# Two experts of a mixture form their second product in rows, both at the end of the order, and the last normalization's work on the vector engine is put elsewhere

## The chip, the core and the metric

The kernel runs on one core of one Trainium2 chip. The metric is the device time of one execution in microseconds (us); of three runs the median counts. In the trace the engines are PE (matrix products, with PEld for its weight loads), DVE (vector work), ACT (activations and scaled copies), POOL and SP; SP starts most of the transfers (DMA), POOL the gathers, the scatters and a few others.

## What is computed

The reference is a trunk of two layers on 512 tokens of width 1024. Each layer is a mixer (sparse attention beside a short convolution) and a feed-forward part, each followed by a residual and a normalization of the rows. The second layer's feed-forward part is a mixture of eight experts, two for each token, and it is the only part that the change touches:

```python
def swiglu(h, wg, wu, wd):
    return (jax.nn.silu(h @ wg) * (h @ wu)) @ wd

def moe_swiglu(h, w_router, wg, wu, wd):
    logits = (h @ w_router).astype(jnp.float32)
    top_v, top_i = lax.top_k(logits, TOP_K)
    w_top = jax.nn.softmax(top_v, axis=-1)
    gate = jnp.sum(jax.nn.one_hot(top_i, N_EXPERTS, dtype=jnp.float32) * w_top[..., None], axis=-2)
    out = jnp.zeros_like(h)
    for e in range(N_EXPERTS):
        out = out + gate[..., e:e + 1].astype(h.dtype) * swiglu(h, wg[e], wu[e], wd[e])
    return out
...
h = layer_norm(ALPHA * h + f, ln2_g[l], ln2_b[l])
```

`wg` and `wu` are 1024 x 1408 and `wd` is 1408 x 1024 for each expert, all in float32: 17.3 MB for an expert.

## The kernel before

The experts are sorted by how many tokens chose them. Expert number e of this order has room for `CAPS[e]` tokens (L28: 160, 168, 152, 144, 136, 132, 128, 128), and `TURN` (L29) says in which order they are worked on: 0, 5, 1, 6, 2, 4, 3, 7. An expert of up to 128 tokens is one chunk of rows, a larger one is two (`chunks`, L33).

For each expert the tokens' rows are fetched from memory by POOL (`gather`, L773) and turned on PE so that the features lie on the partitions (`gather_t`, L783). The weights come in blocks of up to 1 MB that SP loads (`eblock`, L799) into a ring of nine buffers, three called `stage` and six called `estage`. Each block is split into two float16 parts (`split16_ops`, L820): ACT writes the high part `whi` (L824), then DVE the low part `wlo` (L825). The split parts have four buffers each. A product is three matrix instructions (`mm3`, L191: high by high, high by low, low by high), so that 792 instructions do one expert.

The hidden width of 1408 is 11 groups of 128, taken as six and five. A turn of the loop in `moe` (L969 to L1009) runs in this order: the gate product of the first six (`expert_up`, "mm"; four blocks), then what is left of the expert before (`end`), the up product of the first six ("tr"; four blocks), the gate product of the last five (three blocks), the second product over the first six groups (`expert_down`, L869, "s"; three blocks), and the up product of the last five (three blocks). `expert_gate` (L854) and `expert_hidden` (L860) form the hidden values `eg`, `ehh`, `ehl` on ACT and DVE.

`expert_down` holds 128 x 128 of the weights as the stationary operand and moves the tokens past it: 264 instructions for an expert, each as wide as the expert has tokens. So its result lies with the features on the partitions and must be turned back: `expert_end` (L883) copies it out of PSUM with a scale into `yt`, and `expert_out` (L895) makes eight (or sixteen) transposes on PE, scales them by the tokens' gates on ACT into `yr`, and POOL adds these rows to `abuf` in memory (L910). The adds to `abuf` follow each other.

The last expert is treated apart. Once the adds of all others have landed, SP loads all 512 rows of `abuf` into `h` (L984), and POOL fetches the last expert's own rows into `xl` (L985). While its products run, DVE computes the statistics of the rows in `h` (L995, L919; the block stands in program order behind the splits of the second product's first half, so ahead of those of the last up group), and scales them (L925, L926), after which SP stores them. The rows of the last expert get its contribution on DVE (L906), statistics, scaling, and POOL scatters them over the output (L1030). A flag for tokens beyond the room that was kept is read just ahead of that.

The program's order on each engine is a list that a scheduler makes ahead of the run, by the order of the source and its own estimate of when each operand is there; `issue_after(x)` adds that nothing of the block under it stands ahead of x on x's engine. The engines then work strictly down their lists.

Of the kernel before, what the change touches and what calls it, by code (L numbers as in the profile page):

```python
# [7 lines left out]
F32 = mybir.dt.float32  # L8
# [4 lines left out]
AF = mybir.ActivationFunctionType  # L13
OP = mybir.AluOpType
# [14 lines left out]
TURN = (0, 5, 1, 6, 2, 4, 3, 7)  # L29
# [3 lines left out]
def chunks(e):  # L33

    c = CAPS[e]
    return [(0, c)] if c <= 128 else [(0, CH), (CH, c - CH)]

# [12 lines left out]
class Trunk:  # L50
# [698 lines left out]
    def slot_data(self, e):  # L749
# [17 lines left out]
        nc.vector.tensor_reduce(self.sgate[0:n, e, 0:nh], x[:, :, 2:5], axis=AX.X, op=OP.add)  # L767

# [113 lines left out]

    def expert_end(self, e, ys):  # L883
# [11 lines left out]
    def expert_out(self, e, yt, last=None):  # L895
        nc, mp = self.nc, self.mp
        for r, (s, n) in enumerate(chunks(e)):
            yr = None if last is not None else mp.tile([128, D], F32, name="yr", bufs=2)[0:n]
            for half in range(2):
# [3 lines left out]
                c = slice(half * 512, half * 512 + 512)  # L903
                g = self.sgate[0:n, e, r:r + 1]
                if last is not None:
                    nc.vector.scalar_tensor_tensor(last[:, r, c], p[0:n], g, last[:, r, c], op0=OP.mult, op1=OP.add)  # L906
                else:
                    nc.scalar.activation(yr[:, c], p[0:n], AF.Copy, scale=g)
            if last is None:
                nc.gpsimd.indirect_dma_start(out=self.abuf[:, :], in_=yr, in_offset=None, compute_op=OP.add,  # L910
                                             out_offset=bass.IndirectOffsetOnAxis(ap=self.dst[0:n, e, r:r + 1], axis=0))
# [16 lines left out]
    def moe(self, l):  # L928
# [30 lines left out]
        nl, nh = chunks(final)[0][1], len(chunks(final))  # L959
        xl = end[0:nl, 2:2 + nh]  # L960
        mv = mp.tile([128, NT, 2], F32, name="mv4")

        def before_last(tts):

            for tt in tts:
                self.rows_scaled(self.h[:, tt], mv[:, tt, 0:1], rs[:, tt], gb)
                self.store(tt)
        end = None
        for turn, e in enumerate(TURN):  # L969
# [6 lines left out]
            if end is not None:  # L976
                end()
            out = (lambda x=TURN[turn - 1]: self.expert_out(x, self.yt)) if turn else None
# [3 lines left out]
            if last:  # L982
                for tt in range(NT):
                    nc.sync.dma_start(self.h[:, tt], self.abuf[tt * 128:(tt + 1) * 128])  # L984
                self.gather_rows(e, xl, self.abuf)  # L985
# [164 lines left out]
```

## Time and profile before

| | us |
|---|---|
| median of three runs | 1389.82 |
| lowest and highest | 1389.7, 1390.5 |
| profiled execution, its own time | 1391.8 |
| profiled execution, span of its instructions | 1389.8 |

| engine | busy in the span |
|---|---|
| PE | 1339.5 us (96%) |
| DVE | 867.3 us (62%) |
| ACT | 670.0 us (48%) |
| POOL | 75.1 us (5%) |

The mixture takes the time from some 910 us to the end. The busy share of PE counts the pipelined ends of its instructions, so that it tells when PE stands still and not how fast it goes. Times in the rows are microseconds from the start of the span; where several instructions are put together, the second number is the time from the first one's start to the last one's end. What stands in brackets behind an instruction is the idle time of its engine just ahead of it, and what ended that.

### The profile page before, as it was taken

The page shows a single profiled execution, that of the slowest core. Times are in us where ns is not written, and L with a number is a line of the kernel's source. Part 1 is how long each engine was busy: PE and PEld are TensorE (multiplying, and loading weights), DVE is VectorE, ACT ScalarE, POOL GpSimd, SP SyncE. Part 2 cuts the span into 40 slices and gives each one's busy share as a digit, 9 for nine tenths or more (in the row PEclk, how much of TensorE's full clock was granted, in tenths as well). Part 3 has the DMA queues.
Part 4 walks back from the last instruction along what each step waited for, and adds up shares of the span by engine and source line. Part 5 has one row for each costly group of instructions (what it writes and reads, how often), then busy time and mean ns, then how long its engine had stood idle before and what let it go on. Part 6 is the DMA issues. An engine that isn't in the chain of part 4 may idle for free.

```text
span 1389.8 us, 27646 instructions
## 1 busy us (share of the span) xinstructions
PE 1339.5 (96%) x11888; PEld 1181.5 (85%) x11888; DVE 867.3 (62%) x1249; ACT 670.0 (48%) x951; POOL 75.1 (5%) x81
## 2 busy tenths in 40 slices
PE   5999999999999999999999999999999999999974
PEld 5887888898888888888888878889999999999974
DVE  7567665843333332228567665769787788778876
ACT  3575544332322322122565444236777677668761
POOL 3000000000000000000000000101101140011010
PEclk9999999999999999999999999999999999999986
DMA  7442021232322322234442021679999999999961
GB/s 249 128 121 62 31 61 61 91 122 72 110 92 90 121 92 91 91 107 110 130 122 62 32 61 61 211 270 321 327 356 334 323 332 389 337 363 353 343 236 75
DMA packets 135810, 241.16 MB, mean 174 GB/s; under 512 B 10810, under 2 KB 80538, under 8 KB 135684
## 3 DMA queue, kind: packets, MB, share of 16 engines
q1 hardware_dynamic: 131444, 225.28, 47.5%
q0 software_dynamic: 4240, 14.07, 3.7%
q8 instruction: 94, 1.54, 0.5%
q14 instruction: 32, 0.26, 0.1%
HBM read 227.74 MB, written 11.68 MB: 172 GB/s over the span
## 4 chain that ended last, share of the span: by engine, by line
PE 91%; DVE 4%; DMA 2%; ACT 1%; issue 1%; SPq 0%; POOL 0%; POOLq 0%; ACTq 0%
PE mm L198 46%; PE s L198 17%; PE tr L198 11%; PE po L481 3%; PE s L499 2%; PE s L465 2%; PE s L373 1%; PE po L198 1%; PE tr L465 1%; PE tr L499 1%; DVE h L925 1%; PE tr L183 1%; DVE h L926 1%; PE mm L677 1%; PE po L475 1%
## 5 line engine op out<-in xcount | busy, mean ns | idle before, releaser
L198 PEld LDWEIGHTS <-whi 128*128 128x128 f16 x4224 | 342.8, 99 | 2.9 <-issue 2.4
L142 ACT ACTIVATE whi<-stage 128x1024 fp32r<-128x1024 f32 x122 | 127.9, 1058 | 304.8 <-PE mm L198 181.7
L143 DVE TENSOR_TENSOR wlo<-stage,whi 128x1024 fp32r<-128x1024 f32 x118 | 143.7, 1223 | 196.6 <-ACT whi L142 194.4
L198 PE MATMUL mm<-xh,whi 128*128 128x512 f32 (+1 forms) x672 | 257.4, 383 | 0.3 <-DVE e L304 0.3
L198 PE MATMUL mm<-xh,wlo 128*128 128x512 f32 (+1 forms) x672 | 253.0, 377 | 0.4 <-DVE wlo L143 0.4
L198 PE MATMUL mm<-xl,whi 128*128 128x512 f32 (+1 forms) x672 | 252.3, 376 | 0.0
L825 DVE SCALAR_TENSOR_TENSOR wlo<-estage,whi 128x1536 f16<-128x1536 f32 (+4 forms) x106 | 201.6, 1919 | 35.2 <-ACT whi L824 34.9
L198 PEld LDWEIGHTS <-wlo 128*128 128x128 f16 x2112 | 208.6, 99 | 13.2 <-DVE wlo L825 13.2
L824 ACT ACTIVATE whi<-estage 128x1536 f16<-128x1536 f32 (+4 forms) x106 | 170.6, 1613 | 68.8 <-PE s L198 28.0
L198 PEld LDWEIGHTS mm<-xh,wlo 128*128 128x128 f32 x672 | 127.1, 189 | 24.0 <-DVE wlo L143 0.6
L198 PEld LDWEIGHTS mm<-xh,whi 128*128 128x128 f32 x672 | 127.6, 190 | 21.6 <-issue 1.3
L198 PEld LDWEIGHTS mm<-xl,whi 128*128 128x128 f32 x672 | 127.3, 189 | 21.1
L198 PE MATMUL tr<-eh,wlo 128*128 128x128 f16 (+6 forms) x704 | 136.2, 228 | 8.3 <-DVE wlo L825 8.3
L198 PE MATMUL s<-ehh,wlo 128*128 128x128 f16 (+6 forms) x704 | 134.7, 228 | 4.5 <-DVE wlo L825 4.5
L198 PE MATMUL tr<-eh,whi 128*128 128x128 f16 (+6 forms) x704 | 136.3, 229 | 0.0
L198 PE MATMUL tr<-el,whi 128*128 128x128 f16 (+6 forms) x704 | 136.2, 228 | 0.0
L198 PE MATMUL s<-ehh,whi 128*128 128x128 f16 (+6 forms) x704 | 134.7, 228 | 1.1 <-ACT ehh L865 1.1
L198 PE MATMUL s<-ehl,whi 128*128 128x128 f16 (+6 forms) x704 | 134.6, 228 | 1.1 <-DVE ehl L866 1.1
L198 PE MATMUL mm<-eh,whi 128*128 128x128 f16 (+6 forms) x704 | 132.7, 226 | 0.0
L198 PE MATMUL mm<-el,whi 128*128 128x128 f16 (+6 forms) x704 | 132.6, 226 | 0.0
L198 PE MATMUL mm<-eh,wlo 128*128 128x128 f16 (+6 forms) x704 | 132.6, 226 | 0.0
L825 DVE SCALAR_TENSOR_TENSOR wlo<-stage,whi 128x1536 f16<-128x1536 f32 (+5 forms) x56 | 103.0, 1842 | 23.2 <-ACT whi L824 22.2
(302 smaller groups left out, 2220.7 us busy)
## 6 DMA issues: line engine op xcount, KB each, us to landing
estage<-in_moe_wd_dram SPq DMA_DIRECT2D x29, 1024.0 KB, 7.7
stage<-in_w_in_dram SPq DMA_DIRECT2D x32, 512.0 KB, 5.1
estage<-in_moe_wu_dram SPq DMA_DIRECT2D x21, 768.0 KB, 10.5
estage<-in_moe_wg_dram SPq DMA_DIRECT2D x18, 768.0 KB, 7.1
stage<-in_ffn_wg_dram SPq DMA_DIRECT2D x11, 1024.0 KB, 5.2
stage<-in_ffn_wu_dram SPq DMA_DIRECT2D x11, 1024.0 KB, 5.2
stage<-in_ffn_wd_dram SPq DMA_DIRECT2D x11, 1024.0 KB, 4.8
stage<-in_moe_wd_dram SPq DMA_DIRECT2D x11, 1024.0 KB, 9.4
```

The costliest lines, as they stand in the source:

```text
L142: nc.scalar.activation(h, st, AF.Copy)
L143: (eng or nc.vector).tensor_tensor(o, st, h.bitcast(F32), op=OP.subtract)
L183: nc.tensor.transpose(p[:, k * 128:(k + 1) * 128], self.h[:, tt, kk * 128:(kk + 1) * 128], self.ident)
L198: self.nc.tensor.matmul(p, a, b, start=first and n == 0, stop=last and n == total - 1, skip_group_check=shared)
L373: nc.tensor.matmul(ph[r:r + 64, 0:256], e2[kv][:, c].rearrange("p g n -> p (g n)"), w1s[c // 8][:, c % 8], start=c < 2, stop=c > 13, skip_ ...
L465: nc.tensor.transpose(q[:, k * 128:k * 128 + 128], flat[:, c:c + 128], self.ident)
L475: nc.tensor.matmul(po, vbd[r], pct[r, la // 2], start=True, stop=False, skip_group_check=True)
L481: nc.tensor.matmul(po[g * 64:g * 64 + 64, i * 128:i * 128 + 128], v[:, j, c:c + 64], flat[:, k:k + 128], start=False, stop=lbr == 1 and j ...
L499: nc.tensor.matmul(sp[:, wide[i]], qs[:, a, g, qi[i]], keys[:, br, g, 0:wide[i].stop - wide[i].start], start=keys is ks and i == blocks[0] ...
L677: self.nc.tensor.matmul(p, self.h[:, tt, k * 128:k * 128 + 128], self.oh32[:, tt], start=tt == 0 and k % 3 == 0, stop=tt == NT - 1 and (k ...
L824: nc.scalar.activation(hi[:, c], st[:, c], AF.Copy, scale=WS)
L825: self.low = nc.vector.scalar_tensor_tensor(lo[:, c], st[:, c], WS, hi[:, c], op0=OP.mult, op1=OP.subtract)
```

## The change

Experts 6 and 7, the two of exactly 128 tokens, are now the last two of `TURN`, and their second product is made in rows (`expert_down_rows`). There the hidden values of 128 tokens are the stationary operand and the weights move past, 512 columns at a time: 66 instructions of 512 columns instead of 264 of 128. The result has the tokens on the partitions. For expert 6 `expert_rows` scales its two halves out of PSUM, one on ACT and one on DVE, and POOL adds them to `abuf`; `expert_end` and the transposes of `expert_out` are gone for these two. The fixed scale of `expert_end` goes into the gates instead, with one small instruction on DVE in `slot_data`.

For the last expert, the last two blocks of the second product are both split before either is used; then the left half of the columns is finished over both blocks, and then the right one. Each half goes straight from PSUM into `xl` on DVE, with its statistics behind it.

The loads of `h` from `abuf` move from SP's queue to POOL's, right behind the add of expert 6, and the fetch of `xl` goes with them. The statistics of `h` move from in front of the last up group's splits to behind the last of them. The scalings and stores of `h` move from behind the last up group's splits to behind the last split of all, and stand in the source ahead of the left half's instruction on `xl`.

```diff
-TURN = (0, 5, 1, 6, 2, 4, 3, 7)
+TURN = (0, 5, 1, 4, 2, 3, 6, 7)
...
+def by_rows(e):
+    return CAPS[e] == 128
...
+        if by_rows(e):
+            g = self.sgate[0:n, e, 0:nh]
+            nc.vector.tensor_scalar(g, g, 1.0 / (WS * HS * GS * ALPHA), None, op0=OP.mult)
...
+    def expert_down_rows(self, i0, e, f0, n, hh, hl, ys, finish=None):
+        held = []
+        for k0 in range(0, n, 2):
+            k1 = min(n, k0 + 2)
+            src = self.weights("moe_wd", i0, e, slice((f0 + k0) * 128, (f0 + k1) * 128), slice(0, D))
+            hi, lo = self.split16(self.eblock([128, k1 - k0, D], src))
+            held += [(k0 + k, hi[:, k], lo[:, k]) for k in range(k1 - k0)]
+            if finish is not None and 0 < k0 and k1 < n:
+                continue
+            for half, y in enumerate(ys):
+                c = slice(half * 512, half * 512 + 512)
+                for k, h, l in held:
+                    r = slice(k * 128, k * 128 + 128)
+                    for a, b in ((hh, h), (hl, h), (hh, l)):
+                        self.nc.tensor.matmul(y, a[:, r], b[:, c], start=f0 + k == 0 and a is hh and b is h,
+                                              stop=f0 + k == NFE - 1 and b is l)
+                if finish is not None and k1 == n:
+                    finish(half)
+            held = []
+
+    def expert_rows(self, e, ys):
+        nc = self.nc
+        yr = self.mp.tile([128, D], F32, name="yr", bufs=2)
+        g = self.sgate[:, e, 0:1]
+        nc.scalar.activation(yr[:, 0:512], ys[0], AF.Copy, scale=g)
+        nc.vector.tensor_scalar(yr[:, 512:1024], ys[1], g, None, op0=OP.mult)
+        self.add_rows(e, 0, yr)
...
+        def last_rows(half, y):
+            c = slice(half * 512, half * 512 + 512)
+            nc.vector.scalar_tensor_tensor(xl[:, c], y, self.sgate[:, final, 0:1], xl[:, c], op0=OP.mult, op1=OP.add)
+            nc.vector.bn_stats(st2[:, half], xl[:, c])
...
+            if last:
+                for tt in range(NT):
+                    nc.gpsimd.dma_start(self.h[:, tt], self.abuf[tt * 128:(tt + 1) * 128])
+                nc.gpsimd.indirect_dma_start(out=xl, out_offset=None, in_=self.abuf[:, :],
+                                             in_offset=bass.IndirectOffsetOnAxis(ap=self.idx[:, e, 0:1], axis=0))
...
-            if last:
-                for tt in range(NT):
-                    nc.sync.dma_start(self.h[:, tt], self.abuf[tt * 128:(tt + 1) * 128])
-                self.gather_rows(e, xl, self.abuf)
...
+        with self.tc.issue_after(self.low.ins):
+            for tt in range(NT):
+                nc.vector.bn_aggr(mv[:, tt], self.row_stats(self.h[:, tt]))
+            rs = self.small.tile([128, NT, 1], F32, name="rs4")
+            roots(rs, mv)
+            nc.vector.tensor_tensor(self.bad[:, 0:NT], mv[:, :, 1], mv[:, :, 1], op=OP.not_equal)
+
+        def finish(half):
+            if half == 0:
+                with self.tc.issue_after(self.low.ins):
+                    for tt in range(NT):
+                        self.rows_scaled(self.h[:, tt], mv[:, tt, 0:1], rs[:, tt], gb)
+                        self.store(tt)
+            last_rows(half, ys[half])
+        self.expert_down_rows(i0, final, *groups[1], *hid, ys, finish)
...
-        end()
-        self.expert_out(final, self.yt, xl)
```

## Rows read from the trace of the kernel before

**Rows 1.** Page, part 4: the chain that ended last, shares by engine.
```profile
PE 91%; DVE 4%; DMA 2%; ACT 1%; issue 1%; SPq 0%; POOL 0%; POOLq 0%; ACTq 0%
```
**Rows 2.** Stretches: length; busy PE, PEld, DVE, ACT, POOL; clock; DMA share; GB/s.
```profile
1050.00:1100.00 50.00, 49.72 (x714) 49.45 (x712) 38.96 (x34) 33.98 (x31) 7.76 (x4) 1.00 0.92 303
1150.00:1200.00 50.00, 50.00 (x751) 48.85 (x749) 39.73 (x35) 34.54 (x30) 4.07 (x3) 1.00 1.00 360
...
1340.00:1345.00 5.00, 1.64 (x30) 1.47 (x27) 2.64 (x5) 1.38 (x2) 0.00 (x0) 0.95 1.02 399
1345.00:1350.00 5.00, 0.04 (x1) 0.04 (x2) 4.78 (x9) 0.00 (x0) 0.00 (x0) 0.50 0.20 79
1350.00:1355.00 5.00, 5.00 (x50) 5.00 (x51) 5.00 (x8) 2.39 (x3) 0.00 (x0) 0.53 0.00 0
...
1360.00:1365.00 5.00, 0.56 (x4) 0.25 (x3) 5.00 (x6) 0.22 (x2) 0.00 (x0) 0.65 0.40 160
```
**Rows 3.** The chain in order of time, near its end: start, length, what.
```profile
1331.70 4.86 DMA abuf<-yr,dst
...
1337.65 7.55 DMA h<-abuf
...
1345.92 0.11 DVE mv L995
...
1349.96 8.68 PE tr L198 x112
...
1377.72 1.20 DVE st L919 x2
```
**Rows 4.** DVE's instructions in order of time, at the end.
```profile
1345.94 1.24 DVE L919 BATCH_NORM_STATS2 st<-h 128x6 f32<-128x512 f32 x2
...
1352.10 1.48 DVE L825 SCALAR_TENSOR_TENSOR wlo<-stage,whi 128x1280 f16<-128x1280 f32 x1
...
1353.57 2.47 DVE L925 SCALAR_TENSOR_TENSOR h<-h,mv,xl 128x1024 f32<-128x1024 f32 x2
...
1358.67 0.89 DVE L864 SCALAR_TENSOR_TENSOR eg<-tr,eg 128x512 f32<-128x512 f32 x2 [0.23 <-PE tr L198]
...
1367.26 3.42 DVE L825 SCALAR_TENSOR_TENSOR wlo<-estage,whi 128x2048 f16<-128x2048 f32 x2
1375.53 0.69 DVE L890 TENSOR_SCALAR yt<-s 128x512 f32<-128x512 f32 x1 [4.85 <-PE s L198]
1376.20 0.75 DVE L906 SCALAR_TENSOR_TENSOR xl<-mm,sgate,xl 128x512 f32<-128x512 f32 x1
```
**Rows 5.** ACT: high parts of the last turn's first block and of its last up block.
```profile
1292.54 1.48 ACT L824 ACTIVATE whi<-estage 128x1536 f16<-128x1536 f32 x1 [1.73 <-PE s L198]
...
1338.83 1.27 ACT L824 ACTIVATE whi<-stage 128x1280 f16<-128x1280 f32 x1 [0.88 <-PE s L198]
```
**Rows 6.** The chain earlier: PE's pace, by count and length.
```profile
870.44 2.27 PE mm L198 x10
...
1157.09 0.44 PE mm L902 x4
1157.52 0.44 PE po L902 x4
...
1300.94 8.04 PE mm L198 x144
```
**Rows 7.** Adds to `abuf`, by line: POOL ns min/median/max; us from issue to landing.
```profile
L910 POOL DMA_INDIRECT abuf<-yr,dst x13: 1472/2092/12674, 1000.8 to 1331.7; - x13
...
DMA to landing us min/median/max: 4.9/9.1/21.7
```
**Rows 8.** Transfers of 870 to 960: source, queue, count, KB each, median us to landing.
```profile
hbuf<-h POOLq DMA_DIRECT2D x4, 512.0 KB, 4.9
```
**Rows 9.** SP's queue: the start of the last turn's first weight load.
```profile
1271.08 0.37 SPq L806 DMA_DIRECT2D estage<-in_moe_wg_dram  x1
```
**Rows 10.** Transfers of 1150 to 1180: the longest median landing of a weight block.
```profile
estage<-in_moe_wu_dram SPq DMA_DIRECT2D x1, 640.0 KB, 13.1
```

More of the change, by code (lines that the diff above doesn't have):

```diff
@@ L893, in expert_end, with expert_out @@
         return yt[:, 0:KD * cap].rearrange("p (k j) -> p k j", k=KD)
[L895 to L896 removed]
+    def expert_out(self, e, yt):
+        nc = self.nc
         for r, (s, n) in enumerate(chunks(e)):
[L898 removed]
+            yr = self.mp.tile([128, D], F32, name="yr", bufs=2)[0:n]
             for half in range(2):
@@ L902, in expert_out @@
                     nc.tensor.transpose(p[0:n, k * 128:(k + 1) * 128], yt[:, half * 4 + k, s:s + n], self.ident)
[L903 to L911, printed above, removed]
+                nc.scalar.activation(yr[:, half * 512:half * 512 + 512], p[0:n], AF.Copy, scale=self.sgate[0:n, e, r:r + 1])
+            self.add_rows(e, r, yr)
     def store(self, tt):
@@ L958, in moe, with ended @@
         final = TURN[-1]
-        nl, nh = chunks(final)[0][1], len(chunks(final))
-        xl = end[0:nl, 2:2 + nh]
+        xl = end[:, 2]
         mv = mp.tile([128, NT, 2], F32, name="mv4")
[L963 to L968, printed above, removed]
+        st2 = self.small.tile([128, 2, 6], F32, name="st")
+        def last_rows(half, y):
+            c = slice(half * 512, half * 512 + 512)
+            nc.vector.scalar_tensor_tensor(xl[:, c], y, self.sgate[:, final, 0:1], xl[:, c], op0=OP.mult, op1=OP.add)
+            nc.vector.bn_stats(st2[:, half], xl[:, c])
+        def ended(e, hid, ys):
+            if by_rows(e):
+                self.expert_down_rows(i0, e, *groups[1], *hid, ys)
+                self.expert_rows(e, ys)
+                return None
+            self.expert_down(i0, e, *groups[1], *hid, ys)
+            return self.expert_end(e, ys)
+        before = None
         for turn, e in enumerate(TURN):
@@ L975, in moe @@
             gate = self.expert_gate(up("moe_wg", 0))
-            if end is not None:
-                end()
-            out = (lambda x=TURN[turn - 1]: self.expert_out(x, self.yt)) if turn else None
+            yt = before and ended(*before)
+            if last:
[3 more added lines that the diff above has]
+                                             in_offset=bass.IndirectOffsetOnAxis(ap=self.idx[:, e, 0:1], axis=0))
+            out = (lambda: self.expert_out(before[0], yt)) if yt is not None else None
             hid = self.expert_hidden(up("moe_wu", 0, mid=out), gate)
```

27 lines of the change are left out of this document (9 added, 18 removed).

## The prediction

> **What bounds the kernel now.** I read the chain of the page first: PE holds 91% of it [rows 1], so nearly everywhere the question is what PE does, and where it stands still. The stretches answer the second. Through the mixture PE is never idle, at full clock, while the transfers run at 360 GB/s with a share of 1.00: bound by PE, with the memory close behind [rows 2]. Only from 1341.6 on does that break. PE works 0.04 us of the 5 from 1345 and 0.56 of the 5 from 1360, and between them it runs at a clock of 0.53, near the lower level of 1.2 GHz [rows 2].
>
> The chain tells why. The second of two adds to `abuf` begins at 1331.70 and takes 4.86 us; only then are the four loads of `h` let go, and the last needs 7.55 us, to 1345.2 [rows 3]. DVE, which works down its list, waits with the statistics of these rows, and the splits of the last up group stand behind them. PE goes on at 1349.96, after 8.3 us of nothing. The last of these splits (1280 columns) ends at 1352.10 + 1.48 = 1353.6 [rows 4]. I call this point T: everything left on DVE lies behind it. From T to the end of the last statistics of the last expert's rows, 1377.72 + 1.20 = 1378.9 [rows 3], are 25.3 us, and from there to the end of the span 10.9, which the change leaves as they are. So the end has three terms: T, DVE's work from T on, and 10.9.
>
> **Where T goes.** Without statistics ahead, the splits follow the ring of split buffers. ACT's last high part of the up group was released by PE and ran from 1338.83 to 1340.10 [rows 5]; DVE's low part of 1.48 behind it gives 1341.6, if DVE has done the two blocks before by then. PE's release moves as well:
>
> - Expert 6 loses eight transposes: 0.44 + 0.44 = 0.88 us [rows 6].
> - The products in rows have as many columns as before, 264 x 128 = 66 x 512. One of 128 takes 8.04 / 144 = 55.8 ns [rows 6]: 53.3 at one column a clock of 2.4 GHz, and 2.5 besides. For 512 that estimates 216 ns. The nearest row with 512 columns, of another number format, has 2.27 / 10 = 227 [rows 6]. 66 products are 14.2 us at 216 and 15.0 at 227, against 14.7 for 264. I take 216, since here the operands have the format of the 55.8: 0.5 us less for expert 6, 0.3 for the first six groups of the last expert. At 227 it is 0.25 and 0.15 more.
>
> The Trainium skill (TensorE: Matmul & The Clock Gate, section Back-to-back issue gap) has sustained pairs of load and product at 81 ns for 128 columns and 131 for 512. By that the estimate would be 264 x 81 = 21.4 us against 66 x 131 = 8.6. The trace's 55.8 disagrees with the first figure, and no row here goes below 227 for 512 columns.
>
> PE so reaches the end of the second product's first half up to 1.7 us sooner, or 0.5 at the other price. I let T have half of it, as DVE and ACT must keep up: T = 1340.8, between 1339.9 and 1342.2. The order of the experts by itself costs nothing on PE: the same seven precede the last one.
>
> **What DVE does from T on.** Sums of durations; neighbours overlap by some 0.08 us, so about 1 us of waiting is covered:
>
> - statistics of `h`: eight, of which two take 1.24 [rows 4], 5.0; four aggregates of 0.11 [rows 3] and three small ones behind them like these, 0.8. New in this stretch: 5.8
> - the hidden values: 0.89 [rows 4], and as much again for `ehl` on the same shapes: 1.8
> - splits of 2048, 2048 and 1024 columns: 3.42 for 3072 less a third [rows 4], so 3.42 x 5 / 3 = 5.7
> - scalings of `h`: eight, of which two take 2.47 [rows 4]: 9.9
> - the last rows: twice 0.75 [rows 4] and 1.20 for two statistics [rows 3]: 2.7
>
> The sum is 25.9. Before it was 25.3 with the statistics outside, because DVE waited 4.85 us for PE and then had `yt` to write [rows 4]; the four transposes that PE did between are gone too. So the tail stays as long as it was, and the gain is that T comes 12.8 us earlier: **1340.8 + 25.9 + 10.9 = 1377.6**, 12.2 below 1389.8.
>
> **What hides the rest.** PE's last products end under the scalings. After the last split (1340.8 + 5.8 + 1.8 + 5.7 = 1354.1) 18 products of 512 are open: 3.9 us, or 7.7 at the lower clock; the scalings last until 1364.0. The instruction on the left half stands behind all of them in source order, and that exposes 5.9 to 8 us. The up group's 120 products (6.7 us) run to 1346.7, while DVE does the statistics until 1346.6: a near fit. The stores of `h` start in the scalings and have the 10.9 us to land in. The last transfers collide with nothing. The extra instruction in `slot_data` is some 0.15 us of a DVE that was idle for 10 of 50 us [rows 2]. On ACT and DVE expert 6 trades four copies for two.
>
> **The moved transfers.** SP no longer waits for the adds, and nothing but the `xl` fetch and the last scatter is queued behind the loads on POOL. The add of expert 6 now is one. The last turn's first product ends at 1308.98 before [rows 6]; here it is 1.5 later, since the second half of an expert of 144 tokens (7.5 us) is no longer behind it but ahead of it, and that of expert 6 no longer ahead. 30 products of 216 ns and a copy of 0.7 bring the rows to 1317.7. The add takes 4.9 to 21.7, 9.1 in the middle [rows 7]: 1326.8. POOL's load of as many bytes landed in 4.9 [rows 8], against 7.55 on SP [rows 3]; with the fourth load started 2 us behind the first, `h` is there at 1334 to 1336, ahead of T by 5 to 7 us. With the slowest add it is 1348.
>
> **The rivals.**
>
> *Rows that come late.* If `h` is late, DVE waits behind T as it did before. The slowest add of thirteen gives 1348 and costs 7 us: 1385. One add held POOL for 12.7 us where 2.1 is usual [rows 7], so POOL can be held up. The Trainium skill (SBUF — State Buffer, section SBUF: two separate sides) speaks against moving loads to POOL: its transfers wait for descriptors while certain DVE instructions hold a shared port. Five starts on POOL, each behind one split of 2.3 us, would be 11.5 us, `h` at 1346 and the end at 1383. No row shows such a hold for a plain load. Chance 0.10, 1380 to 1386.
>
> *A wrong place in DVE's list.* The scheduler sets the hidden values where it thinks PE is done. If they stand ahead of the statistics, DVE idles from T until PE's 1346.7: 5.9 us, 1383.5. Before, DVE waited 0.23 for them [rows 4], so the estimate was good. Chance 0.09.
>
> *Weights that come late, up to slower than before.* Two experts of 128 tokens now follow each other, and PE asks for weights faster there. A turn of 128 takes 792 x 55.8 ns = 44.2 us and some 2.5 of transposes. The two turns' weights (34.6 MB), two adds and a gather (1.6) and the rows (2.6) are 38.8 MB. A turn's first block is started 21.5 us ahead of its split (1271.08 against 1292.54) [rows 5, 9], so that they have 21.5 + 46.7 and about 42 of the last turn, 110 us. That wants 353 GB/s where 360 was sustained [rows 2]; landings grew to 13.1 us in the turn of expert 6 before [rows 10]. At 345 the end is 2.5 us later, 1380. It decides against the change below 310 GB/s, where 125 us are needed and the 12.2 are gone with 2.8 more; at the slowest row, 303 [rows 2], it is 128 us, 18 more, and the end is at 1396. Against it: 303 stands in a stretch with a share of 0.92, where a large expert asked for no more, and a fifth of the bytes aren't wanted until after T. Chance 0.06 for a few us, 0.07 for slower.
>
> *The scalings out of the way.* If the list has the left half's instruction ahead of them, the last rows follow PE: 1354.1 + 3.9 + 1.35 + 10.9 = 1370, and the scalings with their stores behind need until 1372. Chance 0.08.
>
> *Wide products that cost less than their columns.* PE would reach T sooner, but DVE, busy for 39.73 of 50 us [rows 2], has an idle fifth of the last turn at most to follow with, 8 us of 42: 1370 at best. This is where the rule on pairs would lead. Chance 0.02.
>
> *That it doesn't do what it says.* If the list kept the statistics ahead of the splits, `h` would be there at 1335 without the second add and SP's wait, and PE would stand still for 2 or 3 us instead of 8.3: 1380, still within the forecast. No change at all wants late rows and late weights together: chance 0.04.
>
> **How the numbers follow.** The forecast of 1374.5 to 1380.5 has 0.54: T's bounds of -0.9 and +1.4 and two us for waits between engines. The median of the runs equals the span shown, while the profiled execution as a whole had 1391.8, 2.0 above; I predict the median as the span. The range reaches from the scalings' case, 1371, to most of the late rows, 1384.5. A measurement of this kernel can tell 0.2%, 2.8 us: faster 0.89, same 0.04, slower 0.07.
>
> **What would show it.** Right: no idle of PE over 1 us until some 1346; the last up split ends on DVE at 1340 to 1342; the statistics behind it wait for no transfer; DVE is busy without a gap to the last rows; PE waits for DVE once or twice between 1346 and 1355 and then DVE's scalings outlast PE. Products in rows at 216 ns a piece. Wrong: a wait for `h` behind T, ACT's high parts released by a transfer in the last two turns, or the last rows' instruction ahead of the scalings.

## The result and the profile after

| | before | changed |
|---|---|---|
| median of four runs each, on one chip | 1390.16 us | 1378.31 us |
| lowest and highest | 1389.7, 1394.01 | 1376.29, 1380.98 |
| profiled execution, its span | 1389.8 | 1374.5 (own time 1376.29) |
| PE busy | 1339.5 | 1331.4 |
| DVE busy | 867.3 | 865.7 |

By the medians it is 11.9 us faster, where 1377.6 us, 12.2 below 1389.8, was forecast. The ratio on record is 0.9904, 95% interval 0.9889 to 0.9919, 13.3 us of 1390. The profiled execution of the changed kernel was the lowest of its four, about 2 us under the median; that matters below.

The stretches of the changed kernel (length; busy PE, PEld, DVE, ACT, POOL; granted clock; DMA share; GB/s), which answer [rows 2]:

```profile
1250.00:1300.00 50.00, 49.66 (x744) 45.19 (x742) 44.14 (x34) 39.64 (x37) 3.59 (x2) 1.00 1.02 379
1300.00:1340.00 40.00, 40.00 (x531) 32.22 (x529) 38.82 (x30) 33.34 (x28) 11.70 (x6) 1.00 1.01 372
1340.00:1345.00 5.00, 4.66 (x84) 4.48 (x81) 4.58 (x11) 3.93 (x3) 0.01 (x1) 1.00 0.49 174
1345.00:1350.00 5.00, 0.00 (x0) 0.00 (x0) 5.00 (x8) 0.91 (x3) 0.00 (x0) 0.98 0.00 0
1350.00:1355.00 5.00, 4.23 (x10) 1.29 (x11) 5.00 (x8) 0.54 (x2) 0.00 (x0) 0.50 0.01 3
1355.00:1360.00 5.00, 5.00 (x20) 2.06 (x19) 5.00 (x5) 0.00 (x0) 0.00 (x0) 0.84 0.52 210
1360.00:1365.00 5.00, 0.39 (x2) 0.00 (x0) 4.93 (x9) 0.29 (x1) 0.00 (x0) 0.85 0.52 210
```

PE is busy through to 1344.7, where it had fallen idle at 1341.6 before, and the column to read after that is DVE's: 4.58 of 5, then 5.00 three times and 4.93. From 1340 on DVE is the bound. PE still has its hole, in 1345 to 1350, and works on behind it at the lower of its two levels, 1.2 GHz (0.50).

DVE's instructions at the end of the changed kernel (start, length, what; in brackets the idle time ahead of it), which answer [rows 4]:

```profile
1337.64 1.48 DVE L833 SCALAR_TENSOR_TENSOR wlo<-stage,whi 128x1280 f16<-128x1280 f32 x1
1339.04 1.87 DVE L955 BATCH_NORM_STATS2 st<-h 128x6 f32<-128x512 f32 x3
...
1342.00 0.70 DVE L955 BATCH_NORM_STATS2 st<-h 128x6 f32<-128x512 f32 x1 [0.42 <-DMA h<-abuf]
...
1344.53 2.27 DVE L833 SCALAR_TENSOR_TENSOR wlo<-estage,whi 128x2048 f16<-128x2048 f32 x1
1346.84 2.24 DVE L833 SCALAR_TENSOR_TENSOR wlo<-estage,whi 128x2048 f16<-128x2048 f32 x1
1349.00 0.88 DVE L872 SCALAR_TENSOR_TENSOR eg<-tr,eg 128x512 f32<-128x512 f32 x2
...
1351.94 2.47 DVE L961 SCALAR_TENSOR_TENSOR h<-h,mv,xl 128x1024 f32<-128x1024 f32 x2
...
1361.51 1.40 DVE L1001 SCALAR_TENSOR_TENSOR xl<-s,sgate,xl 128x512 f32<-128x512 f32 x2
1362.83 1.27 DVE L1002 BATCH_NORM_STATS2 st<-xl 128x6 f32<-128x512 f32 x2
```

T, the end of the last up split, is 1339.1 here; the last statistics end at 1364.1, 25.0 us on; the end of the span is 10.4 behind that. Between T and the last rows DVE stands still once, 0.42 us, for a part of `h`.

### The profile page after: what moved, and what is told of

Same layout as the page of the kernel before. It is cut to its first block, busy times and chain, and to the rows that moved or that the text cites. A ratio compares the mean times of both kernels' runs of the same rounds, so it can differ in the third digit from the quotient of the medians.

```text
span 1374.5 us, 26819 instructions
## 1 busy us (share of the span) xinstructions
PE 1331.4 (97%) x11476; PEld 1156.4 (84%) x11476; DVE 865.7 (63%) x1250; ACT 668.4 (49%) x948; POOL 76.5 (6%) x85
## 4 chain that ended last, share of the span: by engine, by line
PE 90%; DVE 4%; DMA 2%; ACT 2%; issue 1%; SPq 0%; POOL 0%; POOLq 0%; ACTq 0%; DVEq 0%
PE mm L203 46%; PE s L203 16%; PE tr L203 10%; PE po L486 3%; PE s L504 2%; PE s L470 2%; PE s L378 1%; PE po L203 1%; PE tr L470 1%; PE tr L504 1%; PE s L906 1%; DVE h L961 1%; DMA abuf<-yr,dst 1%; DVE h L962 1%; DMA h<-abuf 1%
## 5 line engine op out<-in xcount | busy, mean ns | idle before, releaser
L203 PEld LDWEIGHTS <-whi 128*128 128x128 f16 x3872 | 311.5, 98 | 1.2
L203 PEld LDWEIGHTS <-wlo 128*128 128x128 f16 x1936 | 189.1, 98 | 0.0
L203 PE MATMUL tr<-eh,whi 128*128 128x128 f16 (+6 forms) x704 | 133.0, 226 | 0.0
L203 PE MATMUL tr<-eh,wlo 128*128 128x128 f16 (+6 forms) x704 | 133.0, 226 | 0.0
L203 PE MATMUL tr<-el,whi 128*128 128x128 f16 (+6 forms) x704 | 133.0, 226 | 0.0
L832 ACT ACTIVATE whi<-stage 128x1536 f16<-128x1536 f32 (+5 forms) x56 | 86.8, 1551 | 40.2 <-PE tr L203 15.6
L203 PE MATMUL s<-ehl,whi 128*128 128x160 f16 (+5 forms) x528 | 102.6, 228 | 0.0
L203 PE MATMUL s<-ehh,whi 128*128 128x160 f16 (+5 forms) x528 | 102.6, 228 | 0.0
```

The lines of the kernel that those rows point to most:

```text
L203: self.nc.tensor.matmul(p, a, b, start=first and n == 0, stop=last and n == total - 1, skip_group_check=shared)
L832: nc.scalar.activation(hi[:, c], st[:, c], AF.Copy, scale=WS)
```

## The experiments

Each ratio is to the kernel before on the same chip, with its 95% interval; where gains of different kernels are compared, they are these ratios times 1390 us. The changed kernel stands at 0.9904 and, measured again below, at 0.9895.

**The moves alone, and the rows alone.** The kernel before with nothing but the statistics and the scalings put elsewhere:

```diff
-            if last:
-                with self.tc.issue_after(self.low.ins):
-                    for tt in range(NT):
-                        nc.vector.bn_aggr(mv[:, tt], self.row_stats(self.h[:, tt]))
...
             hid = self.expert_hidden(up("moe_wu", 1, mid=mid), gate)
             if last:
                 with self.tc.issue_after(self.low.ins):
-                    before_last(range(NT))
+                    for tt in range(NT):
+                        nc.vector.bn_aggr(mv[:, tt], self.row_stats(self.h[:, tt]))
...
                 self.expert_down(i0, e, *groups[1], *hid, ys)
+                if e == final:
+                    with self.tc.issue_after(self.low.ins):
+                        before_last(range(NT))
```

> The kernel before with one part of the change alone: statistics behind the last up group's splits, scalings behind all splits. Old order of experts, second products in columns, loads of h on SP behind two adds. Theory (DVE's list: the end is T + DVE's work from T + about 10.5): T falls to 1341 to 1342 as no statistics stand ahead of it; h lands at 1345, so DVE waits 2 to 4 us behind T; the list then is that of the changed kernel plus yt and a wait for four transposes (2 us). End near 1379, 10 to 11 us faster than before. Rival (products): the gain comes from the products in rows and the transposes that are gone, so this kernel gains under 4 us. Rival (SP's queue): the gain comes from weight loads that no longer wait behind the adds, so this kernel, whose loads stay on SP, gains under 4 us.

Measured: 1380.82 us, ratio 0.9919 (0.9906 to 0.9931). The other half of the change, the changed kernel with statistics and scalings at their old places in the source:

```diff
+            if last:
+                with self.tc.issue_after(self.low.ins):
+                    for tt in range(NT):
+                        nc.vector.bn_aggr(mv[:, tt], self.row_stats(self.h[:, tt]))
...
             hid = self.expert_hidden(up("moe_wu", 1, mid=mid), gate)
             before, xs = (e, hid, ys), nxt
         with self.tc.issue_after(self.low.ins):
             for tt in range(NT):
-                nc.vector.bn_aggr(mv[:, tt], self.row_stats(self.h[:, tt]))
...
+                self.rows_scaled(self.h[:, tt], mv[:, tt, 0:1], rs[:, tt], gb)
+                self.store(tt)
         def finish(half):
-            if half == 0:
...
             last_rows(half, ys[half])
```

> The changed kernel with the statistics put back in front of the last up group's splits and the scalings back in front of the last second product's splits; rows, order of experts and the loads on POOL as changed. Theory (DVE's list): h lands at 1342 as in the changed kernel, the statistics end at 1344.6, three splits of 5.6 us follow, T is 1350, and some 21 to 23 us of DVE and PE and 10.5 follow: 1382 to 1385, 5 to 8 us faster than before and 6 to 8 slower than the changed kernel. Rival (products) and rival (SP's queue): 10 us or more faster than before, near the changed kernel.

Measured: 1385.4 us, ratio 0.9955 (0.9943 to 0.9968). DVE's lines of the first kernel, then of the second:

```profile
1340.80 1.48 DVE L825 SCALAR_TENSOR_TENSOR wlo<-stage,whi 128x1280 f16<-128x1280 f32 x1
1345.13 0.69 DVE L919 BATCH_NORM_STATS2 st<-h 128x6 f32<-128x512 f32 x1 [1.65 <-DMA h<-abuf]
1365.97 0.68 DVE L890 TENSOR_SCALAR yt<-s 128x512 f32<-128x512 f32 x1
1368.07 1.28 DVE L919 BATCH_NORM_STATS2 st<-xl 128x6 f32<-128x512 f32 x2
```

```profile
1337.46 1.29 DVE L955 BATCH_NORM_STATS2 st<-h 128x6 f32<-128x512 f32 x2 [3.86 <-DMA h<-abuf]
1340.00 0.69 DVE L955 BATCH_NORM_STATS2 st<-h 128x6 f32<-128x512 f32 x1 [1.25 <-DMA h<-abuf]
1348.06 1.48 DVE L833 SCALAR_TENSOR_TENSOR wlo<-stage,whi 128x1280 f16<-128x1280 f32 x1
1371.46 0.69 DVE L1002 BATCH_NORM_STATS2 st<-xl 128x6 f32<-128x512 f32 x1
```

Both expectations held in the main, and the two halves don't add up: 11.3 and 6.3 us by themselves, 13.3 together. In the second kernel the statistics stand ahead of the up splits, and T waits for `h` (5.1 us of waits are left, T = 1349.5 against 1353.6 before). By the profiles an earlier `h` so gives 4.1 us, and 2.7 more lie behind T, where DVE waits 2.2 us less for PE and has no `yt` to write. With the statistics behind those splits DVE waits only 1.65 us for `h`, and an earlier `h` has little left to give. Rows, order and POOL's queue together are worth what lies between 0.9919 and the changed kernel's 0.9904 and 0.9895, some 2 to 3 us, and the intervals overlap; no run here divides it among the three.

**What the scalings hide.** The changed kernel without the eight scalings of `h` (left out of the output too):

```diff
                     for tt in range(NT):
-                        self.rows_scaled(self.h[:, tt], mv[:, tt, 0:1], rs[:, tt], gb)
                         self.store(tt)
```

> The changed kernel without the eight scalings of h: all rows but those of the last expert are stored as they were loaded. It measures what the scalings cost on the path. The prediction held that PE is done 5.9 to 8 us before the scalings are, so this would be 6 to 8 us faster than the changed kernel (1370 to 1372). What the trace of the changed kernel shows speaks for less: PE's last product ended at 1360.2 and the last scaling at 1361.5, since PE itself was held back by DVE's list until 1350; by that it is 1 to 2 us faster (1376 to 1377).

Measured: 1376.13 us, ratio 0.988 (0.9865 to 0.9894), some 2 to 3 us less than the changed kernel by its two ratios, under half of the 6 to 8 of the prediction's working and a little over the other reading. DVE's instruction on the left half, its waits for `h` (us in total, times, longest), and two stretches of this kernel:

```profile
1361.36 0.75 DVE L1001 SCALAR_TENSOR_TENSOR xl<-s,sgate,xl 128x512 f32<-128x512 f32 x1 [6.56 <-PE s L906]
```

```profile
DVE st L955 <- DMA h<-abuf: 3.3, 3, 1.1
```

```profile
1350.00:1355.00 5.00, 1.46 (x4) 0.28 (x5) 4.80 (x9) 0.86 (x3) 0.00 (x0) 0.50 0.00 2
1355.00:1360.00 5.00, 5.00 (x14) 1.84 (x13) 0.00 (x0) 0.00 (x0) 0.00 (x0) 0.54 0.01 3
```

DVE loses 9.6 us of work and gets back 7.0 as waits for PE (6.56 ahead of the left half, 0.46 ahead of the right), which starts its last products at 1353.17, at the lower level. That leaves 2.6 us, as measured. The 3.3 us of waiting for `h` behind T are this execution's own and put DVE and PE back alike. In the changed kernel's profile PE ends 1.1 us ahead of the scalings, not the 5.9 that the prediction saw.

**POOL's queue.** The changed kernel with the loads of `h` back on SP, where they stand behind the last turn's first up weights:

```diff
             yt = before and ended(*before)
-            if last:
-                for tt in range(NT):
-                    nc.gpsimd.dma_start(self.h[:, tt], self.abuf[tt * 128:(tt + 1) * 128])
...
             if turn + 2 < NE:
                 self.slot_data(TURN[turn + 2])
+            if last:
+                for tt in range(NT):
+                    nc.sync.dma_start(self.h[:, tt], self.abuf[tt * 128:(tt + 1) * 128])
```

> The changed kernel with the loads of h back on SP's queue, behind the up product of the first six groups; the fetch of xl stays on POOL. Theory (DVE's list): only the landing of h counts, and only if it lies behind T. The add of expert 6 landed at 1330.1 and POOL's loads at 1342; SP's last took 7.6 us before, so h is there at 1338 and DVE's wait of 0.4 us is gone. Last weight block waits for the add until 1330 and is wanted at 1343: hidden. Within 1 us of the changed kernel, and if the spread of its runs (1376 to 1381) comes from h landing late, a smaller spread. Rival (SP's queue): 4 us or more slower than the changed kernel.

Measured: 1379.61 us, ratio 0.9916 (0.9901 to 0.993). SP's queue there, and ACT's high part of the last up block:

```profile
1328.50 1.80 SPq L1027 DMA_DIRECT2D h<-abuf  x4
1330.55 0.39 SPq L814 DMA_DIRECT2D stage<-in_moe_wu_dram  x1
```

```profile
1337.93 1.27 ACT L832 ACTIVATE whi<-stage 128x1280 f16<-128x1280 f32 x1 [3.94 <-DMA stage<-in_moe_wu_dram]
```

Nothing waits for `h` any more, but the last up weights stand behind SP's wait for the add, ACT waits for them, and DVE for ACT: 2.00 us ahead of T (1340.7) instead of 0.42 behind it. The median is 1.2 to 1.3 us above the changed kernel's two, by the ratios 1.7 to 2.9: more than the expected 1, less than the rival's 4, and the intervals overlap. A gain of POOL's queue isn't shown by the time. The spread of the runs, 1377.1 to 1383.9, isn't smaller either.

**The same kernel again.**

> The changed kernel once more, on the same chip as the three that follow: 0.988 to 0.992 of before. Its runs spread over 4.7 us (1376.3 to 1381.0); if the spread comes from h landing behind T, a slow execution shows DVE waiting for the loads of h for some us.

Measured: 1378.42 us (1375.66 to 1380.27), ratio 0.9895 (0.9878 to 0.9911). Its profiled execution took 1380.27 us, 4.0 more than the first one, and shows T at 1343.3, the last statistics' end 24.5 later and a tail of 10.7, with no wait for `h` at all. So what sets these two executions apart is not `h`; it arises ahead of T. The same two groups of products in the chain, first profile and second:

```profile
973.17 5.29 PE tr L203 x75
1085.27 5.54 PE tr L203 x75
```

```profile
974.16 6.94 PE tr L203 x75
1087.98 7.06 PE tr L203 x75
```

The same 75 products took 1.65 and 1.52 us longer; 0.99 us had gone before them. These sum to 4.2, the whole shift of T. No wait in those stretches names a releaser, but the clock differs. The first group again, first profile and second, with the columns of the stretches above:

```profile
973.17:978.46 5.29, 5.29 (x78) 5.29 (x79) 1.97 (x5) 1.90 (x3) 1.89 (x2) 1.00 0.86 267
```

```profile
974.16:981.10 6.94, 6.94 (x78) 6.94 (x79) 1.98 (x5) 1.91 (x3) 1.89 (x2) 0.75 0.80 235
```

The granted clock was 1.00 in the first profile. In the second it was 0.50, the lower level, from 976 to 978, and 1.00 again from 979; before it fell, PE had made the transposes of the next expert's rows and the group's first 14 products, as it had in the first. In the second group it was 0.78 against 1.00. The other profiles agree: this first group took 5.29 us at a clock of 1.00 in ten of the thirteen, and 6.53 and 6.94 us at 0.81 and 0.75 in the kernels with the statistics behind all splits and with the scalings ahead of the last splits. So the 3.2 us of the two groups are the clock's; why it fell behind the same instructions in one execution and not in another is open. A profile of one execution so fixes a term behind T to some 0.5 us, but T itself only to 4.

**Statistics behind all splits.** The block of statistics goes into `finish`, ahead of the scalings:

```diff
-        with self.tc.issue_after(self.low.ins):
-            for tt in range(NT):
-                nc.vector.bn_aggr(mv[:, tt], self.row_stats(self.h[:, tt]))
...
         def finish(half):
             if half == 0:
                 with self.tc.issue_after(self.low.ins):
+                    for tt in range(NT):
+                        nc.vector.bn_aggr(mv[:, tt], self.row_stats(self.h[:, tt]))
...
                     for tt in range(NT):
                         self.rows_scaled(self.h[:, tt], mv[:, tt, 0:1], rs[:, tt], gb)
                         self.store(tt)
```

> The changed kernel with the statistics of h put behind all splits, like the scalings. DVE's work from T on is the same, only its order is another: the three last splits and the hidden values come first, so that PE starts its last 30 products some 4 to 5 us sooner (1346 instead of 1350.4) and at the full clock, and ends near 1353 instead of 1360. Theory (DVE's list: the sum of its work sets the end): within 1.5 us of the changed kernel. Rival (PE's last products set the end, as the run without scalings suggests): 4 us or more faster than the changed kernel.

Measured: 1379.1 us, ratio 0.9902 (0.9886 to 0.9918): no difference. A stretch of PE and its last product there, and DVE's first instruction on the last rows:

```profile
1350.00:1355.00 5.00, 4.88 (x24) 2.24 (x24) 5.00 (x13) 0.89 (x1) 0.00 (x0) 1.00 0.01 3
```

```profile
1356.01 0.38 PE L906 MATMUL s<-wlo,ehh 128*128 128x512 f16 x1
```

```profile
1359.66 0.74 DVE L1001 SCALAR_TENSOR_TENSOR xl<-s,sgate,xl 128x512 f32<-128x512 f32 x1
```

The hidden values now come early, PE waits 2.5 us instead of 5.7, stays at full clock and is done at 1356.4, although T was 2.3 later than in the changed kernel's profile. The end doesn't move with it: from T to the last statistics' end are 25.7 us, of which 0.98 are waits for ACT. The sum of DVE's work decides, and PE's hole costs nothing. The 2.3 us by which T is later are there at the end of the second group of 75 products, ahead of all that the edit moves.

**The last rows ahead of the scalings.** The kernel above, with the scalings and stores traced behind the scatter of the last rows, so that the scheduler may fill them in. The stores of `h` so come after the scatter, and the last expert's part is missing from the output, in this kernel and the next:

```diff
         def finish(half):
...
-                    for tt in range(NT):
-                        self.rows_scaled(self.h[:, tt], mv[:, tt, 0:1], rs[:, tt], gb)
-                        self.store(tt)
...
             nc.gpsimd.indirect_dma_start(out=self.out[0], out_offset=bass.IndirectOffsetOnAxis(ap=i, axis=0), in_=xl[:, r],
                                          in_offset=None, bounds_check=S - 1, oob_is_err=False)
+        with self.tc.issue_after(held["low"]):
+            for tt in range(NT):
+                self.rows_scaled(self.h[:, tt], mv[:, tt, 0:1], rs[:, tt], gb)
+                self.store(tt)
```

> As the kernel with the statistics behind all splits, and the last rows' instructions with their whole chain come ahead of the scalings in the source; scalings and stores of h fill DVE's gaps and end it. Theory (DVE's list): three scalings (3.6 us) lie behind the flag, the last scatter starts near 1364 instead of 1367.6, and the last scaling ends at 1367 as before with a store of 2.7 behind it: 2 to 4 us faster than the changed kernel. If DVE's sum were not the bound, it would be 6 us or more.

Measured: 1382.37 us, ratio 0.9932 (0.9917 to 0.9946): 4 to 5 us slower than the changed kernel, and neither expectation. The scatter on POOL, the stores in SP's queue, and the longest wait ahead of them (waited for: us in total, times, longest):

```profile
1367.21 1.87 POOL L1071 DMA_INDIRECT out_dram<-xl,dst  x1 [25.45 <-DVE flag L1067]
```

```profile
1371.39 2.90 SPq L950 DMA_DIRECT2D out_dram<-h  x4
```

```profile
SPq L950 <- DMA out_dram<-xl,dst: 3.7, 1, 3.7
```

The scatter starts at 1367.21, against 1367.59 in the changed kernel's profile. T was 1.75 later here, so from T it is 2.1 us sooner, where 3.6 were expected; three scalings do lie behind the flag. But the stores, which write the same output, wait until the scatter has landed. What I had not counted is that in this program the two writers of the output follow each other, so that the scalings are better hidden in front of the scatter.

**One tile on ACT and POOL.** On top of that kernel, one of the four tiles is normalized by ACT (scale and bias) and POOL (two products with rows) instead of DVE:

```diff
+                x = self.h[:, tt]
+                if tt > 2:
+                    nc.scalar.activation(x, x, AF.Identity, scale=rs[:, tt], bias=nm[:, tt])
+                    nc.gpsimd.tensor_tensor(x, x, gb[:, 0], op=OP.mult)
+                    nc.gpsimd.tensor_tensor(x, x, gb[:, 1], op=OP.add)
+                else:
+                    self.rows_scaled(x, mv[:, tt, 0:1], rs[:, tt], gb)
```

> As the kernel with the last rows first, and one of the four tiles of h is scaled by one instruction on ACT and two on POOL, which are idle there (2.84 us each on POOL by the four splits it did in the first layer). Theory (DVE's list): 2.4 us of DVE's work are gone, so 1 to 2.4 us faster than the kernel with the last rows first. Rival (POOL in the way): the last scatter waits on POOL behind the two instructions, and they hold DVE up: no faster, or slower.

Measured: 1388.82 us, ratio 0.9979 (0.9971 to 0.9988), 6.4 us slower than the kernel without it. POOL, then DVE:

```profile
1363.68 3.30 POOL L1081 TENSOR_TENSOR h<-h,xl 128x1024 f32<-128x1024 f32 x1 [18.96 <-ACT h L1080]
1367.06 3.39 POOL L1082 TENSOR_TENSOR h<-h,xl 128x1024 f32<-128x1024 f32 x1
```

```profile
1364.71 2.29 DVE L1057 TENSOR_TENSOR bad<-mv 128x1 f32<-128x1 f32 x1
1368.31 3.23 DVE L961 SCALAR_TENSOR_TENSOR h<-h,mv,xl 128x1024 f32<-128x1024 f32 x1
```

A comparison of 128 numbers, 0.15 us in the kernel above, took 2.29 and ended with POOL's first product, at 1367.0; a scaling of 1.27 took 3.23 and ended 1.1 us, nearly its own length, behind POOL's second. What DVE was to save it lost in these two, 4.1 us; the flag stands behind them, and the scatter started at 1373.08, 5.9 us later than above, of which 1.7 lie ahead of this stretch (the left half's instruction began at 1357.01 instead of 1355.30). T was 2.95 us later than above, and as much was there at the first group of 75 products (977.87 instead of 974.93), so that the 1.7 come from ahead of the edit. The medians differ by 6.4; only 4.1 of it is explained.

**The old order.** The changed kernel with `TURN = (0, 5, 1, 6, 2, 4, 3, 7)`, POOL's loads and fetch behind the two adds of expert 3:

```diff
-TURN = (0, 5, 1, 4, 2, 3, 6, 7)
+TURN = (0, 5, 1, 6, 2, 4, 3, 7)
```

> The changed kernel with the old order of the experts (6 fourth, 3 last but one), so that the two adds of expert 3 with its 144 tokens stand just ahead of the loads of h on POOL. Theory: the order is what lets h be there at T. Two adds one after the other end at about 1336 to 1338 as in the kernel before, POOL's loads land 7 to 11 us later, so h is complete at 1344 to 1348, and DVE stands still for 4 to 8 us behind T (1339 to 1341) with the statistics, everything else as in the changed kernel: 1382 to 1386, and the trace shows waits for h of that sum on DVE. Rival: the order gives nothing, since the loads overlap the splits and the changed kernel's own h was just in time anyway: within 1.5 us of the changed kernel, 1377 to 1380.

Measured: 1378.5 us, ratio 0.9902 (0.9886 to 0.9917): the rival held. The adds in the chain, and DVE's first statistics:

```profile
1319.90 8.47 DMA abuf<-yr,dst
1329.11 7.30 DMA abuf<-yr,dst
```

```profile
1341.87 1.97 DVE L955 BATCH_NORM_STATS2 st<-h 128x6 f32<-128x512 f32 x3 [1.50 <-DMA h<-abuf]
```

The loads start at 1336.70 instead of 1330.38, but by then the weights are nearly all there, and they land in 6.2 us in the middle instead of 9.7. Of 6.3 us DVE sees 1.1 more of waiting than in the changed kernel's first profile.

**The scalings ahead of the last splits.** The changed kernel with the scalings and stores right behind the statistics:

```diff
             nc.vector.tensor_tensor(self.bad[:, 0:NT], mv[:, :, 1], mv[:, :, 1], op=OP.not_equal)
+            for tt in range(NT):
+                self.rows_scaled(self.h[:, tt], mv[:, tt, 0:1], rs[:, tt], gb)
+                self.store(tt)
         def finish(half):
-            if half == 0:
...
             last_rows(half, ys[half])
```

> The changed kernel with the scalings and stores of h left in front of the splits of the last second product (right behind the statistics), which stay behind the last up split. Theory: DVE's sum is the same, but PE gets its last operand 9.9 us later, so the last split ends at 1339.0 + 5.8 + 9.9 + 1.8 + 5.7 = 1362 and 18 products of 512 columns are then open, 3.9 us at full clock and 7.7 at the lower one, with DVE idle: the last statistics end 3 to 7 us later than in the changed kernel, 1381.5 to 1385.5. Rival: if the placement of the scalings gives nothing (PE keeps up, only the first term T counts), it is within 1.5 us of the changed kernel, 1377 to 1380.

Measured: 1380.1 us, ratio 0.991 (0.9895 to 0.9925), 0.8 to 2.1 us slower than the changed kernel by its two ratios, which the intervals don't separate, and just between what the theory and the rival gave. The trace does a little better:

```profile
1354.02 2.29 DVE L833 SCALAR_TENSOR_TENSOR wlo<-estage,whi 128x2048 f16<-128x2048 f32 x1
1361.00 3.42 DVE L833 SCALAR_TENSOR_TENSOR wlo<-estage,whi 128x2048 f16<-128x2048 f32 x2
1366.52 0.75 DVE L1001 SCALAR_TENSOR_TENSOR xl<-s,sgate,xl 128x512 f32<-128x512 f32 x1 [2.10 <-PE s L906]
```

From T (1342.3) to the last statistics' end are 27.2 us, 2.2 over the changed kernel's first profile, of which 2.10 are this wait. It is less than 3 to 7 because the scheduler put the first split between the scalings, so that PE had less open at the end. The place of the scalings is worth some 2 us. That leaves 9 or 10 of the moves' 11.3 for that of the statistics, by subtraction: no run moves them alone.

**Two tiles' statistics on ACT.** The kernel with the statistics last, the mean and the mean square of two tiles summed on ACT:

```diff
-                    for tt in range(NT):
+                    for tt in range(2):
                         nc.vector.bn_aggr(mv[:, tt], self.row_stats(self.h[:, tt]))
+                    with self.tc.issue_after(self.high.ins):
+                        for tt in range(2, NT):
+                            nc.scalar.activation(end[:, 3], self.h[:, tt], AF.Copy, scale=1.0 / D, accum_out=mv[:, tt, 0:1])
+                            nc.scalar.activation(end[:, 3], self.h[:, tt], AF.Square, scale=D ** -0.5, accum_out=mv[:, tt, 1:2])
```

> The kernel with the statistics behind all splits (1379.1 against 1378.4 for the changed kernel), with the mean and the mean square of two of the four tiles of h summed on ACT, which is idle there, by four activations of 128 x 1024. Theory (DVE's sum from T on sets the end): DVE loses four statistics of 0.62 and two aggregates and gains two small instructions, 2.4 us less: 1376 to 1377, with PE's last products ended at 1356 to 1358, ahead of the instructions that read them. Rival (PE or ACT sets the end): no gain or a loss, 1378 to 1381, since ACT's activations of about 1.1 us stand around the high part of the hidden values for which PE waits.

Measured: 1380.02 us (1377.96 to 1382.06), ratio 0.9912 (0.9897 to 0.9927). From T (1341.8) to the last statistics' end (1365.2) are 23.4 us, 2.4 less than in the kernel it is made from, as worked out. The median doesn't show it. In the profile, which is of its lowest time, T comes 2.7 us later than in the first profile of the changed kernel, and all of that is there at the first group of 75 products (975.86 instead of 973.17), long before the edit. So the saving behind T is shown by the trace, and in the time it is lost in the spread ahead of T: no version is shown to beat the changed kernel.

## Why the prediction was right

**The three terms.** T, DVE's work from T and the tail were put at 1340.8, 25.9 and 10.9. The two profiles of the changed kernel have 1339.1, 25.0, 10.4 and 1343.3, 24.5, 10.7. The mechanism is the one that was forecast; that the median came out 0.7 us from the forecast is in part luck, as T was off by -1.7 and +2.5 and the other two terms were too long. T's bounds of -0.9 and +1.4 were too narrow on both sides, since they counted the steps of the change and not the 4 us by which the same program moves ahead of T, most of it by the granted clock. DVE's sum was 0.9 to 1.4 too long: it added durations that overlap by 0.08 each and kept the difference for waits, of which there were 0.42 and none.

**Where the gain comes from.** That it is the statistics leaving the splits of the up group is shown by the moves alone: T falls from 1353.6 to 1342.3 in that kernel's profile, and it gains 11.3 of the 13.3 us, some 2 of them by the place of the scalings. The steps on products and transposes in T are right in size (66 products of 216 ns, below) but no run shows their 0.8 us: they lie under the spread.

**What hides PE's last products.** This step failed. It had the hidden values ready with the statistics and PE done 5.9 us or more before the scalings. In the list `eg` stands behind the statistics and two of the three splits. The rival with a chance of 0.09 had named this place in the list, but the other way round: it feared the hidden values too early, with DVE idle for them. They came late, DVE had other work ahead of them, and PE stood idle and began again at the lower clock:

```profile
PE s L906 <- ACT ehh L873: 5.7, 1, 5.7
```

Its last product started at 1360.01 and took 0.38; the left half's instruction stood ready at 1361.51. The cover was 1.1 us, not 5.9. Without the scalings 2 to 3 us are gained and not 6 to 8, so that in this order of the list the 1371 of the prediction's case of the scalings out of the way isn't reached. With the statistics last the cover is 3.3 us and the time the same, so the failed step cost nothing.

**The moved transfers.** The add began at 1318.64, where 1317.7 was worked out, and then both landings were longer than the rows I took. The end of the chain in the changed kernel, and the landings of the four loads:

```profile
1318.64 11.44 DMA abuf<-yr,dst
1331.55 10.43 DMA h<-abuf
```

```profile
DMA to landing us min/median/max: 7.1/9.7/11.2
```

The add took 11.4 us against 9.1, and the loads 9.7 in the middle against 4.9 from [rows 8]. That row was misread: `hbuf<-h` is a store of rows to memory, not a load, and each went out with one or two stores to `abuf`. It was no price for four loads that go out within 2.25 us beside weights at over 370 GB/s. `h` was there at 1342.0 instead of 1334 to 1336, and the margin of 5 to 7 us was gone, down to a wait of 0.42: one of the prediction's own signs of being wrong, in small. It cost next to nothing because the first tiles came in time and DVE takes them one by one. In the kernel without scalings the loads landed in 11.5 us in the middle and DVE waited 3.3 us for them, so the rival of late rows was nearer than these two profiles show.

The rival's hold on POOL didn't show on the four loads: their starts took 2.25 us in all beside DVE's splits. It did on the fetch of `xl` behind them:

```profile
1332.93 7.08 POOL L1024 DMA_INDIRECT xl<-abuf,idx  x1 [0.30 <-issue]
```

In the kernel with the rows alone, where DVE stood still for `h` from 1333.59, the fetch at 1332.89 took 1.59. In both it ended 0.9 us behind a split of DVE, as it did in every other profile of the changed kernel and of the kernels made from it. `xl` isn't wanted before 1361, so this cost nothing. The Trainium skill's warning (SBUF — State Buffer, section SBUF: two separate sides), that transfers on POOL wait for their descriptors while certain DVE instructions hold a shared port, so agrees with the trace for the fetch and doesn't bear on the four plain starts. The lock between instructions of the two engines, of which the same section tells, agrees with the 2.29 and 3.23 us above.

**Weights.** In the two turns of 128 tokens the memory gave 379 and 372 GB/s where 353 were asked; so 360 was no ceiling. PE didn't wait for them.

**The products in rows.** 216 ns each at full clock, as estimated, and not 227: the first 36 of expert 6 in the chain took 7.77 us.

```profile
1285.58 7.77 PE s L906 x36
```

The Trainium skill's sustained 131 (TensorE: Matmul & The Clock Gate, section Back-to-back issue gap) doesn't hold for this stream, in which each product has a load of its own stationary operand; the same section's formula for a single product, N/2.4 + 2.5, gives the 216.

## What to carry to other kernels

Work that must wait for a late transfer belongs behind everything that another engine waits for, and when two edits shorten the same wait, expect little more than the larger of their gains and not the sum: here 11.3 and 6.3 gave 13.3. Where an engine works down a list without a gap to the end, its sum from the last outside event decides, and holes in the others, or an operand that comes a few us earlier, are worth nothing. Take landing times from rows with the same direction and the traffic that will be there, and a term that lies ahead of the change from more than one execution. When the same instructions take longer with no wait beside them, look at the granted clock of that stretch first.

## What was not expected of the hardware

- A product of 512 columns took 216 ns at a granted clock of 1.00 and 427 at 0.50 (in the changed kernel nine of them lie between the starts 1352.20 and 1356.04), so in rows the lower level costs the full factor of two.
- Two DVE instructions took 2.1 and 2.0 us longer beside products of POOL. Each of these took 3.3 to 3.4 us for 128 x 1024 numbers where DVE takes 1.27; as each began within 0.15 us of a DVE instruction of that length, part of it may be a wait of its own.
- The same 75 products took 1.5 to 1.65 us longer in one execution than in another, at two places, with no wait in the trace: the granted clock was 0.75 and 0.78 there instead of 1.00. Why it fell is open.
- The start of one indirect fetch held POOL for 7.08 us, to 0.9 us behind the last of DVE's splits.
- Four loads of 512 KB on POOL landed in 9.7 us in the middle beside the weights, and in 6.2 where these ran out.
